# A two-layer diffusion backbone: the second mixer's weights split and spilled to DRAM during the first FFN, loaded ready-made later

## Chip, core and metric

The kernel runs on one core of a Trainium2 chip, as one program in one launch. The metric is device time in microseconds (us), the median of the runs shown. The engines' names in the profile are PE (TensorE matmul), PEld (its weight load), DVE (VectorE), ACT (ScalarE), POOL (GpSimd) and SP (SyncE, which issues the DMAs of the kernel before).

## The reference

Two layers work on 512 latent tokens and 256 context tokens of width 1024. Layer 0 has a mixer of attention and a short convolution, layer 1 a bidirectional state-space mixer (SSD); each is followed by a gated FFN with a convolution of width 3. Cut to what bears on the change:

```python
def _conv_ffn(h, w_up, conv_w, w_down):             # w_up 1024 x 5632, w_down 2816 x 1024
    u = _dwconv(h @ w_up, conv_w)
    act, gate = jnp.split(u, 2, axis=-1)
    return (jax.nn.silu(act) * gate) @ w_down

def _mixer_ssd(hs, ..., w_in, ..., w_out, need_out):  # w_in 1024 x 5184, w_out 2048 x 1024
    z, xbc, dt = jnp.split(hs @ w_in, [SSD_INNER, SSD_INNER + SSD_CONV_DIM], axis=-1)
    ...                                              # convolution, two scans, gate by silu(z), norm
    return y @ w_out, hf, hb
```

In layer 1 the output for the context is not needed, so its FFN runs on 512 tokens, that of layer 0 on 768.

## The kernel before

**Arithmetic.** Every float32 product is made of three float32r products: `split` (line 154) writes the high part of a tile on ACT (a copy that rounds) and the low part on DVE (source minus high part), and `mm3` (line 133) issues high x high, high x low and low x high. So each weight tile is loaded as float32 into a raw buffer (`raw`, a ring of four slots of 1024 columns in the arena F), and `loadw` (line 163) then splits it into a slot of 2 x 1024 columns in the arena R. A job's matmuls read that slot. `W` is the ring of such slots, three in both FFNs and in the second mixer.

**Stages.** `mixer0`, `ffn(0)`, `mixer1`, `ffn(1)` follow each other. In `ffn(0)` (line 855) 44 `up` products of 48 matmuls run in 22 pairs, with `down` (line 935) after each group of two to four pairs. Each `up` copies PSUM on ACT (`y`, 128x768), adds two taps on DVE (line 110) and calls `self.pump(2)` (line 325), which takes up to two tiles of the next layers' modulation: a DMA and one or two DVE multiply-and-sum passes (line 259). `up` rotates through four PSUM slots (`self.P`).

**The second mixer's weights.** They are one tile of 512 columns (`ssd_dt`), 24 of 1024 (`ssd_w`, "x", "b" and "c" features), 16 (`ssd_z`) and 16 (`ssd_o`, the output projection), 57 in all. `mixer1` loads them with `loadw` 65 times, since the eight `ssd_o` tiles of the second half are used for tokens 0 and 1 and again for 2 and 3. The calls are at `wdt`, `heads`, `feat_job`, `gate_job` and `wo`. `fill` spreads these jobs among the steps of the scan. `decay` loads (`a_dram`) and the `y_dram` stores and loads go through the same SP queue.

**Order.** A scheduler places every instruction on its engine ahead of the run, from its own estimates; on the chip each engine then takes its instructions in that order and waits where an operand is not ready. `gwr` (two slots of 1024 columns) holds the residual's gate rows before and after the FFN and is free while the FFN runs.

Of the kernel before, what the change touches and what calls it, by code (L numbers as in the profile page):

```python
# [8 lines left out]
F32 = mybir.dt.float32  # L9
F32R = mybir.dt.float32r  # L10
# [8 lines left out]
NT = NL + NC  # L19
# [23 lines left out]
def ring(arena, off, size, n):  # L43
    return Ring(arena, [off + j * size for j in range(n)], size)
# [49 lines left out]
class Kern:  # L94
# [54 lines left out]
    def loadw(self, src, n, rg, pat=None, **dims):  # L149
# [4 lines left out]
        self.split(r, hl[:, :n], hl[:, n:])  # L154
        return hl[:, :n], hl[:, n:]

    def small(self, n):
        r = self.smallr[n]
        r.append(r.pop(0))
        return r[-1]  # L160
# [36 lines left out]
    def build(self):  # L197
        tc = self.tc
        with ExitStack() as ctx:
# [11 lines left out]
            self.ad = dram.tile([32, 1024], F32, name="a_dram")  # L211
            self.gd = dram.tile([8, D], F32, name="g_dram")
            self.yd = dram.tile([2 * D, NL], F32, name="y_dram")
            b = Bump(self.F, 0, self.NF)
            self.cst = b(159)
            self.ident, self.mh, self.one = self.cst[:, :128], self.cst[:, 128:152], self.cst[:, 152:153]
# [639 lines left out]
    def ffn(self, l):  # L856
        io, R, F, fb = self.io, self.R, self.F, self.fb
# [16 lines left out]
        tmp = b.ring(NT, 4)  # L874
        xr = Ring(F, [b.o, b.o + 1024, tb, tb + 1024], 1024)
        th = ring(F, tb + 2048, 512, 2)
        groups, p = [], 0
        for g in (2, 2, 3, 3, 3, 3, 2, 4):
            groups.append(list(range(p, p + g)))
# [25 lines left out]
        def up(j):  # L905
            if j in head:
                ps = head[j][1]
            else:
                ps = self.P(n)
                self.gemm_fm(ps, getw(j), hT, segs=segs)  # L910
                i = seq.index(j) + 1
                if i < len(seq):
                    getw(seq[i])
            wc = self.fcw[:, l * 132 + 3 * j:l * 132 + 3 * j + 3]
            y = tmp(n)
            self.act(y, ps, scale=wc[:, 1:2])
            self.taps(y, ps, wc, segs)
            if j not in head:
                self.pump(2)
            return y  # L920

        wds = {}
# [12 lines left out]
        def down(gi):  # L935
            grp = groups[gi]
            for t in range(ntt):
                ps = self.P()
                for h in range(2):
                    for p in grp:  # L940
                        g = gt[p % 4]
                        self.mm3(ps[:, h * 512:(h + 1) * 512],
                                 [g[:, i * n + t * 128:i * n + (t + 1) * 128] for i in range(2)],
                                 [w[:, h * 512:(h + 1) * 512] for w in wds[p]], p == grp[0], p == grp[-1])
                if gi == 0:
                    self.act(macc[t], ps, AF.Copy)
                elif gi < len(groups) - 1:
                    self.tt(macc[t], ps, macc[t], ALU.add)
                else:
                    for h in range(2):  # L950
                        m = macc[t][:, h * 512:(h + 1) * 512]
                        self.tt(m, ps[:, h * 512:(h + 1) * 512], m, ALU.add)
                if gi == len(groups) - 1:
                    finish(t)
                    if not last and t == 3:
                        self.to_hT(macc[:4], hT, 0, 0, 0, th)
# [29 lines left out]
        for gi in range(len(groups)):  # L986
            nxt = groups[gi + 1] if gi + 1 < len(groups) else []
            for p in nxt[:1]:
                pair(p)
            if not nxt:  # L990
                for c in range(1 if last else 2):
                    self.gate_row(l, 5, c)
                xs = [next_x(t) for t in range(4)]
                self.banks((0, 2, 4), (6, 7))
                self.P.i = 2
            down(gi)
            for p in nxt:
                if p != nxt[0]:
                    pair(p)
                down_w(p)  # L1000
# [4 lines left out]
    def mixer1(self):  # L1005
# [58 lines left out]
            return a.rearrange("p (o d) -> p o d", o=1).to_broadcast([128, m, d])  # L1064


        wdt = self.loadw(io["ssd_dt"], 512, W)
        pdt = self.P(NT)
        heads = {}

# [4 lines left out]
                             [hT(i, k, c0, c1) for i in range(2)], k == 0, k == 7)  # L1075
        dt_gemm(SEGS[:1])
        for j in (0, 1):
            heads[j] = self.loadw(io["ssd_w"][j], 1024, W), self.P(NT)
            self.gemm_fm(heads[j][1], heads[j][0], hT, segs=SEGS[:1])
        self.rest_hT()  # L1080
        dt_gemm(SEGS[1:])
# [63 lines left out]
        def feat_job(j, key, fm, segs=SEGS):  # L1145
            n = segs[-1][1]
            st = {}

            def piece(i):
                def run(w):  # L1150
                    if i == 0:
                        st["ps"] = self.P(n)
                    self.gemm_fm(st["ps"], w, hT, segs=segs[i:i + 1])
                    if i == len(segs) - 1:
                        pend[key] = feat_conv(j, st["ps"], fm, segs)
                return run
            return Job(lambda: self.loadw(io["ssd_w"][j], 1024, W), [piece(i) for i in range(len(segs))])

        def feat_conv(j, ps, fm, segs):
            wc = cw[:, 3 * j:3 * j + 3]  # L1160
# [4 lines left out]

        def gate_job(hg):
            def load():
                return [self.loadw(io["ssd_z"][hg, :, kk * 1024:(kk + 1) * 1024], 1024, W) for kk in range(2)]
            key = "z%d" % hg

            def piece(t):
# [164 lines left out]
                self.split(r[:, i * 512:(i + 1) * 512], yk[k + i][:, :512], yk[k + i][:, 512:])  # L1336

        def wo(hf, kk):
            src = io["ssd_o"][kk * 128:(kk + 2) * 128, hf * 512:(hf + 1) * 512]
            return self.loadw(src.rearrange("(k p) c -> p k c", p=128), 1024, W, "p (k c) -> p k c", k=2)  # L1340

        def acc(ps, toks, w, kk):
            for i, t in enumerate(toks):
# [259 lines left out]
```

## Time and profile before

| | |
|---|---|
| median of 3 runs (lowest, highest) | 1969.88 us (1968.69, 1972.29) |
| the profiled execution: time, span | 1978.45 us, 1976.7 us |
| granted TensorE clock, mean | 0.974 |
| PE busy | 1877.5 us, 95% |
| DVE, ACT, POOL busy | 1282.8, 874.2, 398.0 us |
| DMA moved | 226.21 MB, mean 114 GB/s |

The span is cut by stage with the view of busy time by stretch: `ffn(0)` is about 490 to 1000 us, `mixer1` about 1000 to 1620 us. A busy engine that nobody waits for costs nothing; idle time of PE, and time in which PE runs at its lower clock, is what the end depends on.

### The profile page before, as it was taken

The page shows a single profiled execution, that of the slowest core. Times are in us where ns is not written, and L with a number is a line of the kernel's source. Part 1 is how long each engine was busy: PE and PEld are TensorE (multiplying, and loading weights), DVE is VectorE, ACT ScalarE, POOL GpSimd, SP SyncE. Part 2 cuts the span into 40 slices and gives each one's busy share as a digit, 9 for nine tenths or more (in the row PEclk, how much of TensorE's full clock was granted, in tenths as well). Part 3 has the DMA queues.
Part 4 walks back from the last instruction along what each step waited for, and adds up shares of the span by engine and source line. Part 5 has one row for each costly group of instructions (what it writes and reads, how often), then busy time and mean ns, then how long its engine had stood idle before and what let it go on. Part 6 is the DMA issues. An engine that isn't in the chain of part 4 may idle for free. (4 is left out here: it accounts for less than half of the span.)

```text
span 1976.7 us, 26431 instructions
## 1 busy us (share of the span) xinstructions
PE 1877.5 (95%) x10312; PEld 1602.2 (81%) x10312; DVE 1282.8 (65%) x1835; ACT 874.2 (44%) x1402; POOL 398.0 (20%) x450
## 2 busy tenths in 40 slices
PE   7999998899999999999989898999999999999998
PEld 3887787778888888888868788988887788888886
DVE  3332488747998667545476888878687476555564
ACT  4421367545322222322255475766665465233332
POOL 1000124111000000000050667566473110000002
PEclk9899999999999999999989998999999999999999
DMA  8144200143555435221222213222234563223322
GB/s 328 47 166 172 81 25 12 59 172 112 182 164 186 159 111 179 86 64 54 92 91 64 104 60 107 84 99 96 97 118 160 187 211 125 75 96 96 96 86 75
DMA packets 73077, 226.21 MB, mean 114 GB/s; under 512 B 9020, under 2 KB 11512, under 8 KB 72952
## 3 DMA queue, kind: packets, MB, share of 16 engines
q1 hardware_dynamic: 72952, 224.52, 34.1%
q8 instruction: 81, 1.33, 0.3%
q14 instruction: 44, 0.36, 0.1%
HBM read 210.70 MB, written 13.79 MB: 114 GB/s over the span
## 5 line engine op out<-in xcount | busy, mean ns | idle before, releaser
L131 PE MATMUL psum<-arena_r 128*128 128x512 f32 (+2 forms) x9452 | 1792.6, 350 | 53.2 <-ACT arena_r L101 25.8
L131 PEld LDWEIGHTS psum<-arena_r 128*128 128x128 f32 x9452 | 1521.3, 193 | 297.4 <-ACT arena_r L101 32.4
L101 ACT ACTIVATE arena_r<-arena_f 128x512 fp32r<-128x512 f32 (+5 forms) x545 | 419.4, 794 | 630.8 <-PE psum L131 305.7
L113 DVE TENSOR_TENSOR arena_r<-arena_f,arena_r 128x1024 fp32r<-128x1024 f32 (+4 forms) x497 | 482.9, 989 | 329.7 <-ACT arena_r L101 327.6
L113 POOL TENSOR_TENSOR arena_f<-arena_f 128x256 f32<-128x256 f32 (+5 forms) x330 | 311.1, 968 | 228.2 <-ACT arena_f L101 86.1
L107 POOL TENSOR_SCALAR arena_f<-arena_f 128x1 f32<-128x1 f32 (+2 forms) x88 | 36.8, 418 | 1098.3 <-ACT junk L101 989.5
L110 DVE SCALAR_TENSOR_TENSOR arena_f<-psum,arena_f 128x511 f32<-128x511 f32 (+2 forms) x356 | 217.5, 647 | 53.6 <-ACT arena_f L101 52.3
L113 DVE TENSOR_TENSOR arena_f<-psum,arena_f 128x256 f32<-128x256 f32 (+6 forms) x245 | 161.1, 674 | 130.7 <-PE psum L131 116.0
L101 ACT ACTIVATE arena_f<-psum,arena_f 128x512 f32<-128x512 f32 (+2 forms) x217 | 163.9, 765 | 98.6 <-PE psum L131 42.5
L101 ACT ACTIVATE arena_f<-arena_f 128x512 f32<-128x512 f32 (+5 forms) x115 | 81.7, 711 | 127.8 <-DVE arena_f L110 88.5
L113 DVE TENSOR_TENSOR arena_f<-arena_f 128x512 f32<-128x512 f32 (+5 forms) x148 | 108.2, 741 | 37.5 <-ACT arena_f L101 24.0
L139 PE MATMUL psum<-arena_f 128*128 128x128 f32 x596 | 95.8, 283 | 33.8 <-DVE arena_f L107 20.8
L101 ACT ACTIVATE arena_f<-psum 128x512 f32<-128x512 f32 (+9 forms) x135 | 72.1, 547 | 95.3 <-PE psum L131 84.1
L139 PEld LDWEIGHTS psum<-arena_f 128*128 128x128 f32 x596 | 71.2, 143 | 52.8 <-DVE arena_f L107 24.8
L259 DVE SCALAR_TENSOR_TENSOR junk<-arena_f 128x1024 bf16<-128x1024 f32 x80 | 97.6, 1220 | 19.3 <-DMA arena_f<-in_mod_t_dram 18.2
L113 POOL TENSOR_TENSOR arena_r<-arena_f,arena_r 128x768 fp32r<-128x768 f32 (+2 forms) x28 | 50.0, 1803 | 247.3 <-ACT arena_r L101 232.5
L101 ACT ACT_TABLE_LOAD x52 | 66.7, 1283 | 32.9 <-DVE arena_f L110 15.6
L107 DVE TENSOR_SCALAR arena_f<-arena_f 128x512 f32<-128x512 f32 (+4 forms) x97 | 55.2, 610 | 27.9 <-POOL arena_f L113 27.3
L101 ACT ACTIVATE junk<-arena_f 128x512 bf16<-128x512 f32 (+1 forms) x76 | 40.4, 533 | 53.8 <-DVE arena_f L113 39.1
L110 DVE SCALAR_TENSOR_TENSOR arena_f<-arena_f 128x512 f32<-128x512 f32 (+3 forms) x75 | 48.5, 682 | 11.7 <-POOL arena_f L113 5.8
L101 ACT ACTIVATE arena_r<-psum 128x512 fp32r<-128x512 f32 (+2 forms) x72 | 41.0, 591 | 30.0 <-PE psum L139 15.9
L113 DVE TENSOR_TENSOR arena_r<-psum,arena_r 128x512 fp32r<-128x512 f32 (+2 forms) x72 | 47.3, 674 | 9.6 <-ACT arena_r L101 9.3
(25 smaller groups left out, 235.0 us busy)
## 6 DMA issues: line engine op xcount, KB each, us to landing
arena_f<-in_ffn_up_dram SPq DMA_DIRECT2D x88, 512.0 KB
arena_f<-in_mod_t_dram SPq DMA_DIRECT2D x56, 512.0 KB
arena_f<-in_ffn_down_dram SPq DMA_DIRECT2D x44, 512.0 KB
arena_f<-in_mod_dram SPq DMA_DIRECT2D x40, 512.0 KB
arena_f<-a_dram SPq DMA_DIRECT2D x32, 512.0 KB
arena_f<-in_ssd_w_dram SPq DMA_DIRECT2D x24, 512.0 KB
arena_f<-in_ssd_o_dram SPq DMA_DIRECT2D x24, 512.0 KB
arena_f<-in_ssd_z_dram SPq DMA_DIRECT2D x16, 512.0 KB
```

The costliest lines, as they stand in the source:

```text
L101: return self.nc.scalar.activation(out=out, in_=in_, func=func, **kw).ins
L107: (eng or self.nc.vector).tensor_scalar(**kw)
L110: self.nc.vector.scalar_tensor_tensor(out=out, in0=in0, scalar=s, in1=in1, op0=op0, op1=op1)
L113: return (eng or self.nc.vector).tensor_tensor(out=out, in0=a, in1=b, op=op).ins
L131: self.nc.tensor.matmul(out, a, b, start=start, stop=stop)
L139: self.nc.tensor.transpose(out, in_, self.ident)
L259: self.nc.vector.scalar_tensor_tensor(out=self.junk2, in0=r, scalar=1.0, in1=self.cb[c], op0=ALU.mult, op1=ALU.mult, accum_out=o)
```

## The change

`presplit` is a generator over the 57 tiles in the order of their use. For each it issues a load from GpSimd's DMA queue into a `gwr` slot (one tile ahead), splits it on ACT and DVE into one slot of 2048 columns (at `b.o`, behind the FFN's buffers), and stores both halves from GpSimd's DMA queue into the DRAM tensor `ws_dram`. `ffn(0)` takes a step of it after each `up` but the first three, and on every second token tile of the five middle `down` groups; what is left is taken before the last `down`. `mixer1` then loads the 2048 columns (1 MB, the tile `dt` half of it) straight into the `W` slot with `loads`, on SP, and splits nothing.

```diff
+    def presplit(self, slots):
+        g = self.nc.gpsimd
+        todo = list(self.ssd_weights().items())
+        def get(i):
+            if i < len(todo):
+                w, n, k = todo[i][1]
+                r = self.gwr(n)
+                g.dma_start(out=r if k is None else r.rearrange("p (k c) -> p k c", k=k), in_=w)
+                return r
+        nxt = get(0)
+        for i, (key, (w, n, k)) in enumerate(todo):
+            r, nxt = nxt, get(i + 1)
+            hl = slots(2 * n)
+            hr = hl.bitcast(F32R)
+            self.split(r, hr[:, :n], hr[:, n:])
+            g.dma_start(out=self.wsd[i * 128:(i + 1) * 128, :2 * n], in_=hl)
+            yield
+
+    def loads(self, key, n, rg):
+        hl = rg(2 * n)
+        i = self.wsi[key]
+        self.dma(hl.bitcast(F32), self.wsd[i * 128:(i + 1) * 128, :2 * n])
         return hl[:, :n], hl[:, n:]
...
+            self.wsd = dram.tile([57 * 128, 2048], F32, name="ws_dram")
...
+        pre = iter(()) if last else self.presplit(Ring(F, [b.o], 2048))
...
             if j not in head:
                 self.pump(2)
+                next(pre, None)
...
+                if 0 < gi < len(groups) - 2 and t % 2 == 0:
+                    next(pre, None)
...
             if not nxt:
+                for _ in pre:
+                    pass
...
-        wdt = self.loadw(io["ssd_dt"], 512, W)
+        wdt = self.loads("dt", 512, W)
...
-            heads[j] = self.loadw(io["ssd_w"][j], 1024, W), self.P(NT)
+            heads[j] = self.loads(("f", j), 1024, W), self.P(NT)
...
-            return Job(lambda: self.loadw(io["ssd_w"][j], 1024, W), [piece(i) for i in range(len(segs))])
+            return Job(lambda: self.loads(("f", j), 1024, W), [piece(i) for i in range(len(segs))])
...
-                return [self.loadw(io["ssd_z"][hg, :, kk * 1024:(kk + 1) * 1024], 1024, W) for kk in range(2)]
+                return [self.loads(("z", hg, kk), 1024, W) for kk in range(2)]
...
-            src = io["ssd_o"][kk * 128:(kk + 2) * 128, hf * 512:(hf + 1) * 512]
-            return self.loadw(src.rearrange("(k p) c -> p k c", p=128), 1024, W, "p (k c) -> p k c", k=2)
+            return self.loads(("o", hf, kk), 1024, W)
```

Since the order on every engine is made by the scheduler, it moves too. Three places of it follow.

ACT in the later part of `ffn(0)`, before (`arena_f<-psum,arena_f` is the copy `y` of an `up`, `arena_r<-arena_f 128x1024` the split of an FFN weight, `128x768` the silu and the split of a pair):

```order
L101 ACTIVATE arena_f<-psum,arena_f 128x768
L101 ACTIVATE arena_f<-arena_f 128x768
L101 ACTIVATE arena_r<-arena_f 128x1024
L101 ACTIVATE arena_f<-psum,arena_f 128x768
L101 ACTIVATE arena_r<-arena_f 128x768
L101 ACTIVATE arena_r<-arena_f 128x1024
```

The same place now:

```order
L101 ACTIVATE arena_f<-psum,arena_f 128x768
L101 ACTIVATE arena_f<-arena_f 128x1024
L101 ACTIVATE arena_f<-arena_f 128x768
L101 ACTIVATE arena_r<-arena_f 128x1024
L101 ACTIVATE arena_f<-psum,arena_f 128x768
L101 ACTIVATE arena_f<-arena_f 128x1024
L101 ACTIVATE arena_r<-arena_f 128x768
L101 ACTIVATE arena_r<-arena_f 128x1024
```

The rows `arena_f<-arena_f 128x1024` are the splits of `presplit`; each stands between two copies `y` and writes the one slot that the spill before it reads.

POOL during `ffn(0)`, where it had no row before (L188 is the load, L196 the spill):

```order
L188 DMA arena_f<-in_ssd_w_dram 128x1024
L196 DMA ws_dram<-arena_f 128x2048
L188 DMA arena_f<-in_ssd_w_dram 128x1024
L196 DMA ws_dram<-arena_f 128x2048
L188 DMA arena_f<-in_ssd_z_dram 128x1024
L196 DMA ws_dram<-arena_f 128x2048
```

Loads and spills take turns, so a load two tiles on stands behind the spill that waits for DVE.

SP in the output projection, before:

```order
L123 DMA arena_f<-in_ssd_o_dram 128x2x512
L123 DMA g_dram<-arena_f 8x128
L123 DMA arena_f<-in_ssd_o_dram 128x2x512
L123 DMA arena_f<-g_dram 128x1024
L123 DMA arena_f<-in_ssd_o_dram 128x2x512 x8
L123 DMA x_dram<-arena_f 128x1024
L123 DMA arena_f<-in_ssd_o_dram 128x2x512
```

And now:

```order
L123 DMA g_dram<-arena_f 8x128
L123 DMA arena_r<-ws_dram 128x2048 x2
L123 DMA arena_f<-in_ffn_up_dram 128x1024
L123 DMA arena_f<-g_dram 128x1024
L123 DMA arena_f<-in_ffn_up_dram 128x1024
L123 DMA arena_r<-ws_dram 128x2048 x5
L123 DMA x_dram<-arena_f 128x1024
L123 DMA arena_r<-ws_dram 128x2048 x2
```

A load of half the size into a raw slot became a load of 1 MB into the slot that the matmuls read.

## Rows read from the trace of the kernel before

**Rows 1.** Page, part 1: busy time, share of the span, instructions.

```profile
PE 1877.5 (95%) x10312; PEld 1602.2 (81%) x10312; DVE 1282.8 (65%) x1835; ACT 874.2 (44%) x1402; POOL 398.0 (20%) x450
```

**Rows 2.** Busy time by stretch: stretch, its length, engines, granted clock, DMA share, GB/s.

```profile
500.00:640.00 140.00, 140.00 (x751) 121.52 (x751) 130.20 (x207) 42.74 (x48) 0.00 (x0) 1.00 0.56 179
640.00:980.00 340.00, 340.00 (x1817) 294.82 (x1816) 196.44 (x263) 89.81 (x100) 0.00 (x0) 1.00 0.32 101
1050.00:1550.00 500.00, 466.99 (x2910) 418.70 (x2909) 392.06 (x572) 303.77 (x461) 269.38 (x278) 0.95 0.32 104
...
1540.00:1600.00 60.00, 56.65 (x244) 45.39 (x242) 34.13 (x40) 32.08 (x55) 7.62 (x16) 0.94 0.68 229
```

**Rows 3.** Waits of PE, 1000 to 1650 us: total, times, longest.

```profile
PE psum L131 <- ACT arena_r L101: 23.1, 18, 3.9
PE psum L131 <- DVE arena_r L113: 7.6, 10, 1.9
```

**Rows 4.** Groups by form, 490 to 990 us: busy, mean ns, idle before.

```profile
L259 DVE SCALAR_TENSOR_TENSOR junk<-arena_f 128x1024 bf16<-128x1024 f32 x78 | 95.2, 1220 | 19.2 <-DMA arena_f<-in_mod_t_dram 18.2
L113 DVE TENSOR_TENSOR arena_r<-arena_f,arena_r 128x1024 fp32r<-128x1024 f32 x60 | 72.9, 1222 | 75.7 <-ACT arena_r L101 75.6
...
L101 ACT ACTIVATE arena_r<-arena_f 128x1024 fp32r<-128x1024 f32 x59 | 61.8, 1062 | 214.6 <-PE psum L131 174.2 <-DMA arena_f<-in_ffn_up_dram 27.7 <-DMA arena_f<-in_ffn_down_dram 12.8
```

**Rows 5.** Timeline of ACT: copies `y` of the fourth and the last `up`.

```profile
493.29 0.90 ACT L101 ACTIVATE arena_f<-psum,arena_f 128x768 f32<-128x768 f32 x1 [0.29 <-PE psum L131]
...
974.44 0.90 ACT L101 ACTIVATE arena_f<-psum,arena_f 128x768 f32<-128x768 f32 x1 [0.93 <-PE psum L131]
```

**Rows 6.** Timeline of SP: a 512 KB store, and the load that reuses its buffer.

```profile
432.25 0.33 SPq L123 DMA_DIRECT2D x_dram<-arena_f  x1
435.10 0.33 SPq L123 DMA_DIRECT2D arena_f<-in_ctx_dram  x1
```

**Rows 7.** Busy time by stretch, near the start: the highest DMA rate.

```profile
10.00:20.00 10.00, 8.48 (x33) 2.03 (x35) 2.27 (x7) 0.83 (x4) 2.42 (x6) 1.00 1.03 408
```

**Rows 8.** Groups by form, 1050 to 1550 us.

```profile
L113 POOL TENSOR_TENSOR arena_f<-arena_f 128x512 f32<-128x512 f32 x64 | 84.1, 1334 | 35.1 <-DMA arena_f<-a_dram 35.1
L113 DVE TENSOR_TENSOR arena_r<-arena_f,arena_r 128x1024 fp32r<-128x1024 f32 x58 | 81.6, 1407 | 30.9 <-ACT arena_r L101 30.8
...
L101 ACT ACTIVATE arena_r<-arena_f 128x1024 fp32r<-128x1024 f32 x58 | 61.1, 1054 | 19.5 <-PE psum L131 17.0 <-issue 1.2 <-DMA arena_f<-in_ssd_o_dram 1.0
```

**Rows 9.** Timeline of POOL: its small operations.

```profile
424.85 0.56 POOL L113 TENSOR_TENSOR arena_f<-arena_f 128x1 f32<-128x1 f32 x1
```

**Rows 10.** Page, part 3: DMA queues, MB, share of 16 engines.

```profile
q1 hardware_dynamic: 72952, 224.52, 34.1%
q8 instruction: 81, 1.33, 0.3%
```

**Rows 11.** Timelines of ACT and PE: a stall in the scan.

```profile
1429.51 0.42 ACT L101 ACTIVATE arena_r<-arena_f 128x256 fp32r<-128x256 f32 x1 [5.55 <-POOL arena_f L113]
...
1429.98 15.67 PE L131 MATMUL psum<-arena_r 128*128 128x256 f32 x112 [1.40 <-ACT arena_r L101]
```

**Rows 12.** Timelines of SP and ACT: a 512 KB load and its split.

```profile
1553.55 0.37 SPq L123 DMA_DIRECT2D arena_f<-in_ssd_o_dram  x1
...
1557.23 2.01 ACT L101 ACTIVATE arena_r<-arena_f 128x1024 fp32r<-128x1024 f32 x2 [3.42 <-DMA arena_f<-in_ssd_o_dram]
```

**Rows 13.** Timeline of PE in the output projection.

```profile
1558.34 28.30 PE L131 MATMUL psum<-arena_r 128*128 128x512 f32 x110 [2.91 <-ACT arena_r L101]
```

More of the change, by code (lines that the diff above doesn't have):

```diff
@@ L155, in loadw, with ssd_weights @@
         return hl[:, :n], hl[:, n:]
+    def ssd_weights(self):
+        io = self.io
+        src = {"dt": (io["ssd_dt"], 512, None)}
+        for j in (0, 1, 16, 20, 2, 3):
+            src["f", j] = io["ssd_w"][j], 1024, None
+        z = lambda hg: [(("z", hg, kk), (io["ssd_z"][hg, :, kk * 1024:(kk + 1) * 1024], 1024, None)) for kk in range(2)]
+        for hg in range(8):
+            if hg < 6:
+                for j in (2 * hg + 4, 2 * hg + 5):
+                    src["f", j] = io["ssd_w"][j], 1024, None
+            if hg in (0, 2, 4):
+                for j in (17 + hg // 2, 21 + hg // 2):
+                    src["f", j] = io["ssd_w"][j], 1024, None
+            src.update(z(hg))
+        for hf in range(2):
+            for kk in range(0, 16, 2):
+                w = io["ssd_o"][kk * 128:(kk + 2) * 128, hf * 512:(hf + 1) * 512]
+                src["o", hf, kk] = w.rearrange("(k p) c -> p k c", p=128), 1024, 2
+        self.wsi = {k: i for i, k in enumerate(src)}
+        return src
+    def presplit(self, slots):
[19 more added lines that the diff above has]
+        self.dma(hl.bitcast(F32), self.wsd[i * 128:(i + 1) * 128, :2 * n])
+        return hl[:, :n], hl[:, n:]
     def small(self, n):
```

## The prediction

> **What bounds the kernel now.** I read the page's busy shares first: PE is busy 95% of the span [rows 1], so the end moves only where PE waits or where its clock is low. Busy time by stretch then says where that is. From 500 to 980 us, the FFN of layer 0, PE is busy all of the time and the granted clock is 1.00 [rows 2]: nothing can be won there, only lost. From 1050 to 1550 us, the scan of the second mixer, PE is busy 467.0 of 500 us and the clock is 0.95 [rows 2], that is 33 us idle and 0.05 x 500 = 25 us in slow running. This is what the change can win back. PE's waits there name ACT and DVE, with 23.1 and 7.6 us for tiles in the arena that the matmuls read [rows 3]. DVE is the busier of the two, 392 of 500 us, but in the first part of the FFN it is busier still: 130.2 of 140 us [rows 2]. So the change moves work from a stage with a slack PE to one with none, and the question is whether the FFN hides it.
>
> **The change, part by part.**
>
> *Added in the FFN.* 56 tiles of 1024 columns and one of 512 cost 1.062 us each on ACT and 1.222 us on DVE [rows 4], together 60 and 69 us. ACT has room (42.7 of 140 and 89.8 of 340 us busy [rows 2]). DVE has 340 - 196.4 = 144 us free from 640 us on, where some 39 tiles need 48 us. Before 640 us it has 9.8 us free, and 16 tiles need 19.6 us: 9.8 us too many. The modulation passes are fillers (78 of 1.220 us [rows 4]) and can slide to a later place, but the order on DVE is fixed beforehand, so I do not count on all of it.
>
> *The chain of one tile.* There is one slot for the split halves, so split, spill and the next split follow each other, and this cycle must fit the pace of the turns. 41 `up`s and 15 `down` tiles give 56 turns between the fourth copy at 493.3 us and the last at 974.4 us [rows 5]: one turn per 481.1 / 55 = 8.75 us. The cycle is 1.06 (ACT) + 1.22 (DVE) + the spill. A store of 512 KB frees its buffer 2.85 us after it is issued [rows 6]; at the highest rate seen, 408 GB/s [rows 7], another 512 KB takes 1.29 us, so 1 MB takes 4.14 us from SP. What the issue costs on GpSimd no row shows: not below 0, and not above a full pass of 128x512, 1.33 us [rows 8]; it is a job of the sequencer with no tile to read, nearest to POOL's small operations of 0.56 us [rows 9], and I take 0.6. The spill shares the 16 engines with SP's loads, since every queue is counted against the same 16 [rows 10]: its own 2.57 us of transfer grow by the share that is taken, 0.56 or 0.32 [rows 2], by 1.4 or 0.8 us. DVE comes to the tile about half an operation late, 0.6 us where it is full and 0.4 us later. Sum: 1.06 + 1.22 + 4.14 + 0.6 + 1.4 + 0.6 = 9.0 us before 640 us, and 1.06 + 1.22 + 4.14 + 0.6 + 0.8 + 0.4 = 8.2 us after. So the chain falls behind by 0.25 x 16 = 4 us in the first part and keeps up in the second. ACT and DVE take their work in order, so a split that waits for its spill holds the copies, taps and weight splits behind it, and PE stands once its four PSUM slots are full. Because turns come in bunches (three within one `down`), I add 2 us. With the 9.8 us of DVE this makes **+16 us**. The lower bound is 0, all hidden by slots and fillers; the upper one a cycle of 10.2 us throughout (below): 55 x 1.5 = +82 us.
>
> The Trainium skill ("DMA: Bandwidth & Descriptors", section on issuing engines not being separate DMA queues) says that DMAs from GpSimd run on the same 16 engines and interleave with the others, which speaks against a queue of its own as a remedy; the queue rows agree with it in how they count. If the queue had bandwidth of its own, the two sharing terms would fall away, the cycle would be 7.6 us at most and the term +10 us.
>
> *Bandwidth.* 1.57 MB per 8.75 us is 180 GB/s, on top of 179 and later 101 GB/s [rows 2]: 359 and 281 of 408. It fits, so I cost it at nothing beyond the sharing above. If that cover went, SP's weight loads would come late, as they already make ACT wait 40 us there without harm to PE [rows 4].
>
> *Removed in the second mixer.* 64 splits of 1024 columns and one of 512. Of the 58 in the stretch, 1.407 us each on DVE and 1.054 on ACT [rows 8], about 50 are weights: 70 us of DVE's 392, a sixth. A DVE pass there takes 1.407 where the same one takes 1.222 in the FFN with POOL idle [rows 4], so it also hinders POOL and the other way round. Bounds: no gain, since stalls like the one at 1429 us come down a chain that begins on POOL, 5.55 us of ACT's waiting for it [rows 11]; and all 33 + 25 = 58 us. I take a third of the idle time and a fifth of the slow time, 11 + 5: **-16 us**, nearer to the first bound, because the weight splits are fillers there and rarely what PE waits for.
>
> *Loads of 1 MB.* A 512 KB load is used 3.68 us after its issue [rows 12]; 1 MB takes 3.68 + 1.29 = 5.0 us and starts only when the slot is free, where before the data lay ready and 2.3 us of splitting remained. Among the scan's steps two other slots give PE at least one job of 48 matmuls meanwhile, so I cost this at nothing; without that cover each job would start 2.7 us late. It is not covered where the tile of the first "b" features takes the slot of `dt`: **+2 us** (0 to +5). In the output projection a tile serves only 12 matmuls of 28.30 / 110 = 0.257 us [rows 13], 3.1 us; the two that cover a load take 6.2 us, enough for 5.0 us alone, but with a second load under way it can be 5.0 + 2.57. The stretch moves 229 GB/s x 60 us = 13.7 MB [rows 2], and some 17 half-megabytes more make 22.6 MB, 377 of 408 GB/s. Bounds: 0, and 16 x (7.6 - 6.2) = +22 us. I take **+8 us**.
>
> *Head of the mixer.* GpSimd's last spills stand ahead of its small operations for the last tokens' norm. The spill holds GpSimd only until it is issued; nothing.
>
> **Sum.** +16 - 16 + 2 + 8 = +10 us on the profiled execution's 1978.45 us (its span is 1976.7): 1988.5. The median of the runs is 8.6 us lower, so 1979.9, rounded to 1980 us.
>
> **Rivals.**
>
> *The FFN hides it all (faster).* If the cycle is at most 8.75 us everywhere and the modulation passes slide, the +16 goes. Then the mixer decides: -16 + 2 + 8 = -6, up to -58 + 0 + 0. With half of the bound, -29 + 8: 1949 us. For it: PE has no wait in the FFN even where DVE is 93% busy, and slots for three jobs lie between. Against: both the fixed order and the 9.8 us of overfull DVE.
>
> *GpSimd's issue is held up by DVE (much slower).* The DVE pass that takes 1.222 us beside an idle POOL and 1.407 beside a busy one [rows 4, 8] shows that these two hinder each other. If each spill's issue waits for one DVE pass, the cycle is 9.0 + 1.2 = 10.2 us; it decides from 8.75 us on, and 55 x 1.5 = 82 us take the place of the 16: 1980 + 66 = 2046 us. The Trainium skill ("SBUF — State Buffer", section on SBUF's two separate sides) has such a rule: a DVE operation in its two-port mode keeps GpSimd from writing DMA descriptors; for DVE operations with two SBUF inputs, those of this FFN, it names only GpSimd operations that read SBUF, so by that rule this would not happen here.
>
> *It does not take the work off.* Splits go, but waits for 1 MB loads take their place throughout the scan, with decay loads queued behind them on SP: 50 jobs late by 1 us on the mean, no gain: 1980 + 16 + 50 = 2046 us. Against: the jobs between.
>
> *The terms cancel within 4 us.* 1966 to 1974 us.
>
> **How the numbers follow.** A difference of 0.2%, 4 us, is about what a measurement of this kernel can tell from none. The forecast's case, slower by 4 to 56 us, gets 0.42; the slow rivals 0.07 and 0.03; so slower 0.52. Within 4 us: 0.10. Faster: 0.38, mostly between 1940 and 1966. The range from 1942 to 2036 us leaves out the upper two rivals (0.10) and the far end of the gain (0.08). The forecast's own range is 1974 to 2036 us.
>
> **What would show it.** PE in the FFN: idle time of some 10 to 20 us between 500 and 980 us, its waits naming ACT or DVE rows behind a 128x1024 split into the FFN's arena, and those splits waiting for the spill. If the cycle is the cause, splits follow each other about 9 us apart early and 8.2 us later in a phase when they wait. In the scan, PE's idle time should fall from 33 to about 22 us, and the DVE's busy time by some 70 us. In the output projection, PE should wait for the loads from DRAM. I am wrong if PE stays busy in the FFN (then faster), or if the spills take over 6 us from issue to landing (then slower by far).

## The result, and the profile after

The changed kernel takes 1956.64 us (median of 6 runs, 1954.23 to 1959.24), against 1970.57 us (1968.69 to 1972.38, 6 runs) for the kernel before beside it: a ratio of 0.9929, 95% interval 0.9917 to 0.9942. It is faster by 0.7%, about 14 us. I had forecast 1980 us and held "slower" for the likeliest. The profiled execution after took 1959.24 us with a span of 1957.5 us and a mean granted clock of 0.982 (before: 1978.45, 1976.7 and 0.974).

Busy time by stretch of the changed kernel, with the columns and stretches of [rows 2]:

```profile
500.00:640.00 140.00, 140.00 (x752) 121.57 (x752) 133.12 (x199) 56.18 (x60) 14.83 (x28) 1.00 0.86 300
640.00:980.00 340.00, 340.00 (x1816) 294.86 (x1815) 252.74 (x325) 130.51 (x140) 44.25 (x78) 1.00 0.83 292
1050.00:1550.00 500.00, 471.88 (x3014) 423.18 (x3013) 334.17 (x529) 257.67 (x420) 249.68 (x279) 0.98 0.49 176
1540.00:1600.00 60.00, 53.99 (x287) 45.38 (x286) 30.03 (x50) 27.26 (x63) 10.03 (x24) 0.94 0.76 287
```

The FFN carries the new work (DVE 133 and 253 us in place of 130 and 196, DMA share 0.86 and 0.83 in place of 0.56 and 0.32), and PE is still busy all the time at full clock. In the scan DVE lost 58 us of work, PE is busy 472 of 500 us and the clock is 0.98.

A window of fixed times compares different work once one kernel runs ahead, so I cut each trace at marks that every kernel has: the first copy `y` after 478 us on ACT, the transposes `128*8` of the gate columns at the end of the FFN and in the output projection, and the first 64x64 matmul of the second mixer. PE's timeline at the last three, before:

```profile
974.24 0.38 PE L139 MATMUL psum<-arena_f 128*8 128x128 f32 x2
1051.32 0.58 PE L1090 MATMUL psum<-arena_f 64*128 64x64 f32 x6 [0.42 <-ACT arena_f L101]
1547.43 0.27 PE L139 MATMUL psum<-arena_f 128*8 128x128 f32 x1
```

and after:

```profile
974.59 0.38 PE L139 MATMUL psum<-arena_f 128*8 128x128 f32 x2
1056.78 0.58 PE L1146 MATMUL psum<-arena_f 64*128 64x64 f32 x6 [0.42 <-ACT arena_f L101]
1526.19 0.27 PE L139 MATMUL psum<-arena_f 128*8 128x128 f32 x1
```

The lengths between the marks in us, one execution each, for these two and all runs below (the first copy stands at 480 to 485 us in every execution, whatever the change: that much differs ahead of it):

| kernel | FFN | head of the mixer | scan | output projection to the end |
|---|---|---|---|---|
| before | 490.3 | 77.1 | 496.1 | 429.3 |
| the change | 489.6 | 82.2 | 469.4 | 431.3 |
| e1_split_unused | 489.7 | 86.4 | 488.8 | 428.3 |
| e2_no_outproj | 489.7 | 72.7 | 467.8 | 430.6 |
| e3_eight_spilled | 489.7 | 73.0 | 471.9 | 430.5 |
| e5_spill_half_more | 492.1 | 138.7 | 469.5 | 434.8 |
| e6_halves_apart | 497.0 | 72.7 | 467.0 | 432.9 |
| e7_49_tiles | 489.7 | 73.0 | 467.7 | 437.0 |
| e8_dve_back | 489.6 | 112.3 | 469.8 | 427.6 |
| e9_act_back | 489.7 | 99.0 | 471.5 | 431.9 |
| e10_two_slots | 515.8 | 65.8 | 472.7 | 430.0 |
| e11_two_slots_before | 516.8 | 65.5 | 488.2 | 428.6 |
| e12_dve_on_tile | 489.7 | 82.9 | 491.0 | 433.7 |
| e13_act_on_tile | 489.7 | 80.8 | 482.4 | 429.9 |
| e14_gate_rows_raw | 489.6 | 82.9 | 471.5 | 431.7 |
| e15_gate_and_x | 489.7 | 78.9 | 471.6 | 432.4 |
| e16_54_tiles | 489.7 | 72.9 | 467.1 | 433.8 |

So the change costs nothing in the FFN (-0.7), **5.1 us at the head of the mixer**, wins **26.7 us in the scan** and gives back 2.0 us after it. Two other executions with the old loads (e1 and e11) have a scan of 488.8 and 488.2 us, so some 7 of the 26.7 probably belong to this one execution of the kernel before, which took 8 us more than its median.

What the spills did in the FFN, from the view of the tile `ws_dram` on POOL, up to 640 us and from there on (duration of an issue, first and last start):

```profile
L196 POOL DMA_DIRECT2D ws_dram<-arena_f x16: 538/538/622, 485.5 to 634.6; - x16
...
L196 POOL DMA_DIRECT2D ws_dram<-arena_f x41: 538/538/644, 644.6 to 999.3; - x41
```

One tile per 9.9 us in the first part (149.1 / 15), per 8.9 us later (354.7 / 40), 9.18 us on the mean of 56: slower than the turns' 8.75 us, so that the last spill is issued 25 us after the last copy `y`. These are mean distances: only 31 of the 57 splits waited for a spill, the others stood where the order had put them. ACT did wait for the spills, and longer than for anything else there (waits of ACT, 480 to 1000 us: total, times, longest):

```profile
ACT arena_f L101 <- DMA ws_dram<-arena_f: 92.5, 31, 9.3
ACT arena_r L101 <- PE psum L131: 45.2, 18, 5.9
```

Yet the copies that free PE's slots came on time. The last is at 974.79 us, 0.35 us behind that of [rows 5]:

```profile
974.79 0.90 ACT L101 ACTIVATE arena_f<-psum,arena_f 128x768 f32<-128x768 f32 x1 [4.27 <-PE psum L131]
```

What gave way were the modulation passes and the splits themselves. The same group of DVE from 500 to 640 us, before:

```profile
L259 DVE SCALAR_TENSOR_TENSOR junk<-arena_f 128x1024 bf16<-128x1024 f32 x52 | 63.4, 1219 | 3.4 <-DMA arena_f<-in_mod_t_dram 2.9
```

and after, with the new splits below it:

```profile
L309 DVE SCALAR_TENSOR_TENSOR junk<-arena_f 128x1024 bf16<-128x1024 f32 x44 | 53.6, 1219 | 0.2
...
L113 DVE TENSOR_TENSOR arena_f<-arena_f 128x1024 fp32r<-128x1024 f32 x14 | 17.1, 1223 | 3.9 <-ACT arena_f L101 3.9
```

Eight of the 52 passes moved behind 640 us, 9.8 us of DVE's time, as much as my sum had said was too many (it had counted on 16 splits there, and 14 came).

PE's waits from 1000 to 1650 us, against [rows 3]:

```profile
PE psum L139 <- DVE arena_f L107: 14.6, 6, 8.8
PE psum L131 <- DMA arena_r<-ws_dram: 9.5, 6, 3.3
PE psum L131 <- DVE arena_f L113: 8.6, 11, 1.8
PE psum L131 <- ACT arena_r L101: 5.5, 7, 1.4
PE psum L131 <- DVE arena_r L113: 3.8, 7, 1.4
```

The same view of the kernel before has also:

```profile
PE psum L139 <- DVE arena_f L107: 6.5, 4, 3.2
```

The waits for split tiles fell from 23.1 to 5.5 us (ACT) and from 7.6 to 3.8 (DVE). New are 9.5 us for the loads from DRAM, and the wait for the norm of the last tokens (L107), nearly all of it at the head of the mixer, grew from 6.5 to 14.6 us.

### The profile page after: what moved, and what is told of

It reads as the page before. It is cut to its first block, busy times and chain, and to the rows that moved or that the text cites. A ratio compares the mean times of both kernels' runs of the same rounds, so it can differ in the third digit from the quotient of the medians.

```text
span 1957.5 us, 26571 instructions
## 1 busy us (share of the span) xinstructions
PE 1861.5 (95%) x10312; PEld 1588.3 (81%) x10312; DVE 1268.3 (65%) x1827; ACT 868.6 (44%) x1391; POOL 440.3 (22%) x564
## 5 line engine op out<-in xcount | busy, mean ns | idle before, releaser
L131 PE MATMUL psum<-arena_r 128*128 128x512 f32 (+3 forms) x9452 | 1773.4, 348 | 42.7 <-DVE arena_f L113 14.3
L113 DVE TENSOR_TENSOR arena_r<-arena_f,arena_r 128x1024 fp32r<-128x1024 f32 (+5 forms) x432 | 396.4, 934 | 296.0 <-ACT arena_r L101 293.6
L101 ACT ACTIVATE arena_r<-arena_f 128x512 fp32r<-128x512 f32 (+5 forms) x480 | 352.5, 760 | 427.4 <-PE psum L131 164.1
L113 POOL TENSOR_TENSOR arena_f<-arena_f 128x256 f32<-128x256 f32 (+6 forms) x330 | 290.6, 906 | 210.8 <-ACT arena_f L101 57.2
L110 DVE SCALAR_TENSOR_TENSOR arena_f<-psum,arena_f 128x511 f32<-128x511 f32 (+1 forms) x356 | 217.7, 647 | 64.3 <-ACT arena_f L101 61.4
L101 ACT ACTIVATE arena_f<-arena_f 128x512 f32<-128x512 f32 (+5 forms) x172 | 140.9, 825 | 258.5 <-DMA ws_dram<-arena_f 92.5
L113 DVE TENSOR_TENSOR arena_f<-arena_f 128x512 f32<-128x512 f32 (+6 forms) x205 | 178.1, 880 | 70.1 <-ACT arena_f L101 50.6
L107 POOL TENSOR_SCALAR arena_f<-arena_f 128x1 f32<-128x1 f32 (+2 forms) x88 | 35.1, 399 | 587.7 <-ACT junk L101 468.4
L196 POOL DMA_DIRECT2D ws_dram<-arena_f x57 | 31.3, 550 | 462.6 <-DVE arena_f L113 462.6
L139 PE MATMUL psum<-arena_f 128*128 128x128 f32 (+1 forms) x596 | 94.9, 285 | 41.1 <-DVE arena_f L107 28.9
L139 PEld LDWEIGHTS psum<-arena_f 128*128 128x128 f32 (+1 forms) x596 | 70.8, 144 | 58.8 <-DVE arena_f L107 33.7
L107 DVE TENSOR_SCALAR arena_f<-arena_f 128x512 f32<-128x512 f32 (+4 forms) x97 | 55.1, 610 | 30.0 <-POOL arena_f L113 29.3
L110 DVE SCALAR_TENSOR_TENSOR arena_f<-arena_f 128x512 f32<-128x512 f32 (+3 forms) x75 | 48.2, 683 | 30.1 <-ACT arena_f L101 23.0
```

The lines of the kernel that those rows point to most:

```text
L101: return self.nc.scalar.activation(out=out, in_=in_, func=func, **kw).ins
L107: (eng or self.nc.vector).tensor_scalar(**kw)
L110: self.nc.vector.scalar_tensor_tensor(out=out, in0=in0, scalar=s, in1=in1, op0=op0, op1=op1)
L113: return (eng or self.nc.vector).tensor_tensor(out=out, in0=a, in1=b, op=op).ins
L131: self.nc.tensor.matmul(out, a, b, start=start, stop=stop)
L139: self.nc.tensor.transpose(out, in_, self.ident)
```

## The experiments

Each run's ratio is to the kernel before, timed beside it on the same chip (medians 1969.7 to 1970.7 us).

**The price alone.** e1_split_unused: the FFN as in the change, the mixer as before.

```diff
-        wdt = self.loads("dt", 512, W)
+        wdt = self.loadw(io["ssd_dt"], 512, W)
...
-            return self.loads(("o", hf, kk), 1024, W)
+            src = io["ssd_o"][kk * 128:(kk + 2) * 128, hf * 512:(hf + 1) * 512]
+            return self.loadw(src.rearrange("(k p) c -> p k c", p=128), 1024, W, "p (k c) -> p k c", k=2)
```

(and likewise at `heads`, `feat_job` and `gate_job`.)

> All 57 tiles are split and spilled in the FFN as in the change, but the second mixer loads and splits its weights itself, as before; nothing reads what was spilled. So this is the cost of the FFN part alone. Theory (the FFN hides the splits and spills; the tail of their chain delays the head of the mixer): PE 100% busy from 500 to 980 us, the head of the mixer 5 to 6 us late, time 1975 to 1979 us against 1970.6 before. The forecast's reason (the FFN pays 16 us): 1986 us, with PE idle in the FFN. Rival (the late head is an accident of the order of the changed mixer and no price of the chain): 1969 to 1972 us.

Measured: 1975.9 us, ratio 1.0032 (1.0020 to 1.0045). The FFN costs nothing; the head takes 86.4 in place of 77.1 us. So the price is 9.3 us at the head, 5.8 us in the medians, and none of it lies where I had put it.

**The gain alone.** e3_eight_spilled: eight tiles spilled, loaded over and over.

```diff
         todo = list(self.ssd_weights().items())
+        todo = todo[:7] + todo[41:42]
...
-        i = self.wsi[key]
+        i = 1 + self.wsi[key] % 7 if n == 1024 else 0
```

> Only 8 of the 57 tiles are split and spilled in the FFN; the mixer loads 1 MB for every tile as in the change, the same 8 over and over. Left out: 49 splits and spills, so that the weights are not the right ones. This is the gain alone, without the price in the FFN. Theory (FFN free but for the tail): 1950 to 1953 us, 5 us under the change, all of it at the head of the mixer. The forecast's reason (a price of 16 us in the FFN): 1941 us. Rival (no price at all): 1956 us.

Measured: 1944.54 us (0.9865, 0.9846 to 0.9884), 12 us under the change and 5 to 9 us lower than the theory said. The head takes 73.0 us: without a tail it is 4 us *shorter* than before. What this stretch has less is some splits of the mixer's first tiles, which ACT and DVE did while they finished the FFN's tokens (DVE is busy 44.6 us in place of 47.6, ACT 33.0 in place of 34.7); that they make the 4 us was not tried by itself. By these two runs the change's +5.1 us is a price of 9 less a relief of 4.

**Fewer tiles.** e2_no_outproj spills 41 tiles, e7_49_tiles 49, e16_54_tiles 54; the rest of `ssd_o` is loaded and split as before.

```diff
-        todo = list(self.ssd_weights().items())
+        todo = list(self.ssd_weights().items())[:41]
...
-            return self.loads(("o", hf, kk), 1024, W)
+            src = io["ssd_o"][kk * 128:(kk + 2) * 128, hf * 512:(hf + 1) * 512]
+            return self.loadw(src.rearrange("(k p) c -> p k c", p=128), 1024, W, "p (k c) -> p k c", k=2)
```

(e2's edit; e7 and e16 cut the list at 49 and 54 and load the rest of `ssd_o` in the old way.)

> The 16 tiles of the output projection stay as before (512 KB loads, split in the mixer); 41 tiles are split and spilled. The chain ends some 130 us before the FFN does. Theory (the chain's tail costs 5.5 us at the head, the 1 MB loads of the output projection 2 us, and the gain is made in the scan): 1949 us, between 1946 and 1953, with the gate rows loaded before 980 us again. Rival (the output projection's own relief is a part of the gain): 1957 to 1962 us. Rival (the late head has nothing to do with the tail): 1955 us.

> The eight tiles of the second half of the output projection stay as before, 49 are split and spilled, so that the chain ends some 60 us before the FFN does. Theory (only the chain's tail costs): the head as in the run with 41 tiles, time 1945 to 1949 us. Rival (each spill costs something, by the DMA rate or by DVE, tail or not): 1949 to 1953 us, between the run with 41 tiles and the change.

> The last three tiles of the output projection stay as before, 54 are split and spilled. Theory (the chain's end decides, one for one): it ends 25 us earlier, which frees the head as fully as with 41 tiles, 73 us in place of 82.2; the mixed output projection may give back 0 to 5 us, 1947 to 1953 us. Rival (each split in the last 100 us of the FFN costs something): head 78 to 81 us, 1953 to 1956 us.

Measured: 1946.79 us (0.9884, 0.9870 to 0.9897), 1952.64 us (0.9914, 0.9900 to 0.9927) and 1948.30 us (0.9886, 0.9871 to 0.9901). In all three the head takes 72.7 to 73.0 us, so the tail is gone even with 54 tiles, whose last spill is issued at 967.5 us (tile `ws_dram` on POOL):

```profile
L196 POOL DMA_DIRECT2D ws_dram<-arena_f x54: 536/536/622, 481.9 to 967.5; - x54
```

PE's waits from 975 to 1060 us with 41 tiles:

```profile
PE psum L139 <- ACT arena_f L101: 3.4, 1, 3.4
PE psum L131 <- DMA arena_r<-ws_dram: 3.3, 1, 3.3
PE psum L139 <- DVE arena_f L107: 2.6, 2, 2.3
```

The 33 tiles that e2 spills over e3's eight cost nothing that these runs show. With 49 tiles the head is as predicted but the time is the rival's, for another reason: the output projection, whose first half then loads 1 MB per tile and whose second half splits, takes 6 us more than with 41 tiles. Why that mixture is worse than either kind was not tried. The versions with 41 and with 54 tiles beat both kernels, by 1.2% and 1.1% on the one before.

**A longer chain.** e5_spill_half_more stores the high half a second time.

```diff
             g.dma_start(out=self.wsd[i * 128:(i + 1) * 128, :2 * n], in_=hl)
+            g.dma_start(out=self.wsd2[i * 128:(i + 1) * 128, 0:n], in_=hl[:, :n])
```

> Each spill is followed by a second store of its high half (512 KB) to another DRAM tensor, so that the cycle of the one slot grows by 1.3 to 1.8 us, from about 7.8 us (where a split waits for the spill) to 9.1 to 9.6 us, over the pace of the turns of 8.75 us. Theory (the cycle against the pace decides, less what slots hold back, 26 us for three turns): 57 cycles of 9.35 us are 533 us where 494 are there, so 10 to 40 us slower than the change, 1967 to 1997 us, most of it at the end of the FFN and PE waiting there. Rival (fillers and slots hide it at any cycle): under 1962 us.

Measured: 2018.94 us (1.0249, 1.0230 to 1.0268), 62 us over the change and beyond both expectations. The spills run from 483.2 to 1060.3 us, and PE stands almost wholly after the FFN (tile `ws_dram` on POOL; timeline of PE):

```profile
L196 POOL DMA_DIRECT2D ws_dram<-arena_f x57: 533/533/614, 483.2 to 1060.3; - x57
```

```profile
1074.92 0.69 PE L139 MATMUL psum<-arena_f 128*128 128x128 f32 x2 [60.26 <-DVE arena_f L107]
```

The cycle is 577.1 / 56 = 10.31 us, 1.13 over the change's mean; the chain gets 56 x 1.13 = 63 us longer, and 62 us are lost, 56.5 of them at the head and 2.5 in the FFN. The price is one for one, and no slot takes anything off it. Two things were wrong in my expectation: the cycle, which I had put at 9.35 us, and the 26 us that I took off for the slots. (The order put each second store ahead of its spill, since it needs ACT's half alone.)

**A shorter chain.** e6_halves_apart stores the high half as soon as ACT has it.

```diff
-            self.split(r, hr[:, :n], hr[:, n:])
-            g.dma_start(out=self.wsd[i * 128:(i + 1) * 128, :2 * n], in_=hl)
+            self.act(hr[:, :n], r, AF.Copy)
+            g.dma_start(out=self.wsd[i * 128:(i + 1) * 128, :n], in_=hl[:, :n])
+            self.tt(hr[:, n:], r, hr[:, :n], ALU.subtract)
+            g.dma_start(out=self.wsd[i * 128:(i + 1) * 128, n:2 * n], in_=hl[:, n:])
```

> All 57 tiles as in the change, but the two halves of a tile are stored apart: the high half as soon as ACT has written it, the low half after DVE. The next ACT split then waits for a store of 512 KB that began 1.2 us or more earlier, so the chain of 57 gets shorter (56 cycles of 9.18 us = 514 us in the change). Theory (what costs is only how far the chain reaches beyond the FFN, one for one): a cycle shorter by 0.5 us ends the chain 28 us earlier, enough to free the head of the mixer, 1945 to 1949 us, 9 us under the change. Rival (more stores on the same queue and GpSimd, the cycle stays): 1955 to 1960 us.

Measured: 1954.38 us (0.9920, 0.9906 to 0.9935), no clear gain on the change. The cycle shrank to (936.0 - 483.8) / 56 = 8.07 us and the head to 72.7 us, as expected, but the FFN grew by 7.4 us. Busy time of 500 to 640 us in this run, and what PE waited for:

```profile
500.00:640.00 140.00, 135.11 (x719) 116.51 (x719) 126.19 (x186) 56.66 (x62) 25.41 (x48) 0.99 0.89 312
```

```profile
PE psum L131 <- DVE arena_f L110: 4.1, 1, 4.1
```

The tap (L110) came late, but not for want of room on DVE, which is busy 126 us here and 133 us in the change. ACT stood before the split of an FFN weight, whose load SP had issued behind two modulation loads (timelines of SP and ACT):

```profile
600.88 0.33 SPq L123 DMA_DIRECT2D arena_f<-in_ffn_down_dram  x1
```

```profile
609.38 1.06 ACT L101 ACTIVATE arena_r<-arena_f 128x1024 fp32r<-128x1024 f32 x1 [7.81 <-DMA arena_f<-in_ffn_down_dram]
```

The load is used 8.5 us after its issue, where 3.68 us were enough in [rows 12]. Two copies `y` stood behind that split, at 610.34 and 612.81 us, and PE waited for the tap of the second. So the in-order ACT can hold PE up as I had forecast, but what held ACT here was a late weight load (the cover that the prediction's bandwidth term relied on), not a spill. In the change the like load went out ahead of the two modulation loads, at 589.59 us, and ACT waited 1.1 us for it. Whether the faster chain made the load late, at a DMA share of 0.89, or only the new order on SP, was not tried.

**The slots.** e10_two_slots and e11_two_slots_before give PE two PSUM slots in place of four in this FFN, in the change and in the kernel before.

```diff
-        self.P = Ring(self.psa, [512 * j for j in ((4, 6, 0, 2) if last else (6, 0, 2, 4))], 1024)
+        self.P = Ring(self.psa, [512 * j for j in ((4, 6, 0, 2) if last else (6, 0))], 1024)
```

> The change with two PSUM slots in place of four in the FFN of layer 0 (to be read against the kernel before with the same edit), so that PE can be one turn ahead of ACT and DVE in place of three. Theory (the splits go where ACT and DVE have room and hold up the copies by no more than 3 us, as the copies' times show, so that no slots are needed to hide them): no more than 4 us lost on the kernel before with two slots in the FFN, the difference of the two kernels as with four slots, 10 to 18 us. Rival (four slots hide a lag of up to three turns, 26 us): PE idle in the FFN, the change slower than the kernel before, both with two slots.

> The kernel before with two PSUM slots in place of four in the FFN of layer 0: the control of the run above. Both theories: PE may wait a little after the down products, 1970 to 1985 us; what counts is the difference to the run above.

Measured: 1966.20 us (0.9980, 0.9967 to 0.9993) with the change and 1986.71 us (1.0087, 1.0058 to 1.0117) without, 20 us apart, where 10 to 18 were expected. The FFN takes 515.8 us with the change and 516.8 without: with either kernel the FFN is equally long, so at this pace the slots are not what hides the chain. The pace itself is slower here, by 26 us over the FFN, so these runs alone don't rule out that slots help at the old one; there the copies speak, which come at most 3.1 us late, far less than a turn. The head shows something else: with an FFN 26 us longer the chain ends in time, and the head is as short with the change as without, 65.8 and 65.5 us.

**Which relief makes the gain.** e8_dve_back and e9_act_back add one pass per loaded tile on a raw slot alone; e12_dve_on_tile and e13_act_on_tile let the pass read the loaded tile.

```diff
         self.dma(hl.bitcast(F32), self.wsd[i * 128:(i + 1) * 128, :2 * n])
+        r, h = self.raw(n), hl.bitcast(F32)
+        self.tt(r, h[:, :n], h[:, n:], ALU.subtract)
```

(e12; e13 has `self.act(r, h[:, :n], AF.Copy)`, e8 and e9 `self.tt(r, r, r, ALU.subtract)` and `self.act(r, r, AF.Copy)`.)

> The change, with one DVE pass of 128x1024 on a raw slot for each tile that the mixer loads, which no matmul waits for: DVE has again the busy time of the splits, ACT has not. Theory (the 20 to 27 us of the scan come from a DVE that is relieved of a sixth of its work): 10 to 20 us slower than the change, 1966 to 1976 us. Rival (the gain is that a job's matmuls wait for one load instead of a load and two passes): no more than 4 us slower, under 1961 us.

> The change, with one ACT copy of 128x1024 on a raw slot for each tile that the mixer loads, which no matmul waits for: ACT has again the busy time of the splits, DVE has not. Theory (DVE's relief makes most of the gain, ACT's little, since ACT is the less busy one): 2 to 6 us slower than the change, 1959 to 1963 us. Rival (ACT is what PE waited for, 23.1 us of its waits named it before): 10 us or more slower, over 1966 us.

> The change, with one DVE pass of 128x1024 for each tile that the mixer loads, which reads the loaded tile and writes a raw slot that nobody reads: DVE has again the busy time of the splits, at about their place, and the matmuls don't wait for it. Theory (DVE's relief makes most of the gain in the scan): scan 10 to 20 us longer than the change's 469 us, time 1966 to 1977 us. Rival (the gain is that a job waits for a load alone and no longer for two passes): scan under 474 us, time under 1961 us.

> The same with one ACT copy of 128x1024 for each tile in place of the DVE pass. Theory (ACT's relief gives little): scan 1 to 5 us longer than the change's 469 us, time 1958 to 1962 us. Rival (PE's waits of before named ACT with 23.1 us, so that ACT's relief is the larger part): scan 10 us longer or more, over 1966 us.

Measured: e8 1984.34 us (1.0071, 1.0054 to 1.0088) and e9 1970.69 us (1.0000, 0.9987 to 1.0013), but these two tell nothing of the scan. Their passes read nothing that is loaded, so the order put 44 and 39 of the 65 at the head of the mixer (112.3 and 99.0 us), among the work that PE waits for, others ahead of it, and none between 1090 and 1480 us. e12 1981.19 us (1.0059, 1.0034 to 1.0083), scan 491.0 us; e13 1965.70 us (0.9982, 0.9966 to 0.9999), scan 482.4 us. Busy time in the scan, from mark to mark, e12 and e13:

```profile
1053.17:1544.20 491.03, 454.26 (x2888) 407.26 (x2889) 392.19 (x569) 252.98 (x408) 272.63 (x278) 0.97 0.43 156
```

```profile
1051.16:1533.53 482.37, 453.01 (x2888) 406.36 (x2889) 330.25 (x522) 295.12 (x454) 251.97 (x278) 0.97 0.45 160
```

The same stretch in the kernel before:

```profile
1051.32:1547.43 496.11, 463.52 (x2890) 415.86 (x2891) 390.83 (x571) 302.10 (x460) 269.38 (x278) 0.95 0.32 104
```

and in the change:

```profile
1056.78:1526.19 469.41, 446.84 (x2889) 402.58 (x2889) 330.81 (x522) 252.24 (x407) 249.42 (x278) 0.98 0.47 167
```

In this stretch e12 has 47 of the added passes, of 1.393 us each: DVE is as busy as before (392 and 391 us), ACT as little as in the change (253 and 252). A DVE pass whose result nobody reads takes the whole gain back (491.0 against 488 to 496 us with the old loads). The pass reads the loaded tile and could hold its slot against the next load, but PE waits for loads hardly longer than in the change, 4.6 against 3.3 us. So the gain needs DVE's time; the shorter way from load to matmul, which e12 keeps, does not make it.

An ACT copy takes 13 us back, more than the 1 to 5 that the theory gave it, but this is not the price of its busy time alone:

```profile
L101 ACT ACTIVATE arena_f<-arena_r 128x1024 f32<-128x1024 f32 x47 | 49.5, 1054 | 40.6 <-DMA arena_r<-ws_dram 40.5
```

ACT stood 40.5 us before these copies for the loads that they read, where in the kernel before it waited 1.0 us for such loads [rows 8]. How much ACT's relief is worth stays open. The two losses, 22 and 13 us, are together more than the gain, so they are not shares of it.

**By which way the tail costs.** e14_gate_rows_raw puts the FFN's two gate rows into raw slots, e15_gate_and_x also turns the order of the slots of the x rows.

```diff
-        g = self.gwr()
+        g = self.raw() if (l, j) == (0, 5) else self.gwr()
...
-        xr = Ring(F, [b.o, b.o + 1024, tb, tb + 1024], 1024)
+        xr = Ring(F, [tb, tb + 1024, b.o, b.o + 1024], 1024)
```

(the second piece in e15 alone.)

> The change with the FFN's two gate rows in raw slots, so that their loads no longer wait until the last tiles are split out of the gate rows' slots; the last splits and spills stay. Theory (the tail costs through these slots: the load of a gate row holds the SP queue for some 10 us and the finishing of the tokens with it): head of the mixer 74 to 78 us in place of 82.2, 1949 to 1954 us. Rival (the tail costs by its splits' own places on ACT and DVE, or by the slot that the x rows share with the spill): head above 80 us, 1955 to 1959 us.

> As the run above, and the first two rows of x go to the slots of the FFN's copies, the next two to the spill's slot, so that the first x row too waits for no spill. Theory (both shared slots make the price of the tail): head 72 to 75 us, as with 41 tiles, 1945 to 1950 us. Rival (the x slots don't matter): as the run above within 2 us. Rival (the splits' own places): above 80 us, 1955 to 1959 us.

Measured: 1959.66 us (0.9949, 0.9931 to 0.9967) and 1954.80 us (0.9922, 0.9901 to 0.9942); heads of 82.9 and 78.9 us. In the change the gate rows are loaded at 986.4 and 998.0 us, in e14 at 977.7 and 978.2, and nothing is won: my theory of the gate rows fell. What e14 shows in its place is a split among the last that waits for the spill ahead of it on ACT, with the tokens' sums of squares queued behind it:

```profile
985.81 1.06 ACT L101 ACTIVATE arena_f<-arena_f 128x1024 fp32r<-128x1024 f32 x1 [6.68 <-DMA ws_dram<-arena_f]
```

The x rows' slots are worth 3 to 4 us of the 9 (78.9 against 82.2, or against e14's 82.9), the end of the chain before the FFN's end all of it (54 tiles). How the other 6 us divide between the splits' places on ACT and DVE and the spill's slot, which two x rows still share in e15, is not settled.

## Why the prediction was wrong, point by point

**The step that failed** is the +16 us of the FFN, and in it the sentence that a split which waits for its spill holds the copies and taps behind it, so that PE stands. The terms ahead of it were near. The issue took 0.54 us (0.6), the spill 5.9 us to land before 640 us and 5.2 later (5.5 and 4.9 with the sharing), ACT's and DVE's passes 1.06 and 1.22. The cycle was put at 9.0 and 8.2 us; late in the FFN, where one split after another waited (845 to 861 us), they follow each other 7.9 to 8.1 us apart, but on the mean of all tiles it was 9.9 and 8.9, since 26 of the 57 splits did not wait for a spill and came later still, where the order had them. It did fall behind, by more than I said. But a turn does not need the tile of its own time: the order had the late splits at later turns, eight modulation passes moved behind 640 us, and the copies stayed within 3.1 us of their old times all through the FFN, though ACT waited up to 9.3 us at once. So PE lost nothing there (489.6 us against 490.3; e1 489.7). That PE does stand once ACT holds the copies long enough is what e6 shows, for the load of an FFN weight. The four PSUM slots, which I named as the limit, did not decide: no copy came late by a turn. "I do not count on all of it" was the wrong choice for the passes that can slide.

**The head of the mixer, "nothing"**, was the second error, of the other sign: the lag that the FFN did not pay came due there, 9 us by itself (e1), and one us more for each us that the chain gets longer (e5). I had asked only whether GpSimd's issue holds its small operations; the end of the chain holds ACT in its order and the x rows' slot (how much each, the runs leave open). Nor did I see the relief of 4 us in the same place.

**The scan, -16 us:** mechanism right, size too small. From mark to mark PE's idle time fell from 32.6 us (496.11 - 463.52) to 22.6, 10 us where I had taken 11. The other 16.7 us of the 26.7 are PE's busy time for the same matmuls (463.5 to 446.8 us) at a clock of 0.98 in place of 0.95; there I had taken 5. In e1 and e11, with the old loads, PE is busy 455.1 and 453.5 us there, so some 7 to 8 of the 16.7 are the change's, and its gain against these two is about 19 us. The reason for choosing the small end, that the weight splits are fillers and rarely what PE waits for, is what e12 speaks against: a pass whose result nobody waits for costs as much, by its place on DVE ahead of work that PE does wait for.

**The 1 MB loads.** PE waits 3.3 us for one of them right after the head; I had given +2 us (0 to +5) to such a case. In the output projection it waits 6.2 us for five (9.5 less 3.3), and from there to the end 2.0 us are lost, where I had put +8.

**The sum.** -0.7 + 5.1 - 26.7 + 2.0 = -20.3, with 1.0 us ahead of the first copy, against +16 - 16 + 2 + 8. The nearest rival was the one by which the FFN hides it all, at 1949 us. Its condition, a cycle of at most 8.75 us, did not hold; its result did, less the tail: without the tail it is 1947 to 1948 us (e2, e16). That the number fits is in part luck, since its sum of -29 + 8 leaves out the +2 and holds 8 us for the 1 MB loads, which cost 2, and nothing for the head. (The forecast's "slower by 4 to 56 us" does not fit its range either, which runs to 66 us above 1970.)

**The rival of a cycle of 10.2 us** was met in e5, by a second store: 2019 us, where I had 2046, with nearly all of the loss behind the FFN. In the change itself, spills are issued in 0.54 to 0.64 us beside a DVE that is busy 133 of 140 us, so GpSimd's issue is not held up by these passes. The Trainium skill ("SBUF — State Buffer", section on SBUF's two separate sides) lets DVE operations with two inputs in SBUF hinder only GpSimd operations that read SBUF, and the trace agrees.

**What would show it** was named rightly: PE stayed busy in the FFN, which I had put down as the sign that I am wrong and that the kernel is faster. The other sign, spills of over 6 us, said nothing: before 640 us they took 5.1 to 7.4 us to land, and PE stayed busy.

## What to carry to other kernels

When work is moved into a stage that has slack, cost the *end* of the added chain first: lateness inside the stage can slide, what is left at its end is paid one for one. Fit the number of pieces to the stage (54 of 57 here) rather than all of it. Of an engine that takes its work in order, count every pass, also those that nobody waits for.

## What was not expected of the hardware

PE stayed 100% busy at a clock of 1.00 for 480 us while the DMA engines were busy 0.83 to 0.86 of the time at 292 to 300 GB/s, and the splits on ACT and DVE kept their times (1.060 and 1.222 us). A faster chain is not better by itself: the change, with its longer cycle, loses nothing in the FFN, while e6 loses 7 us there.
